# A hybrid recurrent and attention block: early loads at the turn, other places for gates and low parts, and another end

## The chip, the cores and the metric

The kernel runs on one core of one Trainium2 chip. The time is device time in microseconds (us) of one execution; lower is better. Engines are named as in the profile: PE (TensorE matmul), PEld (its weight loads), DVE (VectorE), ACT (ScalarE), POOL (GpSimd), SP (SyncE, here a queue for DMAs only). L154 is line 154 of the kernel before.

## The reference, cut to what matters

One block over 2048 rows of 1024 channels, in float32. From c come shift, scale and gate; h is the normed x. One input projection of h (1024 to 8192) gives eight parts; a recurrent branch and an attention branch each end in a 1024 x 1024 projection; they are merged by sigmoid gates, projected by w_o, added to x under the gate, and normed.

```python
mod = c_act @ w_mod[l] + b_mod[l]
shift, scale, gate = jnp.split(mod, 3, axis=-1)
h = rms_norm(x, g_norm[l]) * (1.0 + scale[:, None, :]) + shift[:, None, :]
x_rnn, z_rnn, q, k, v, z_attn, g_r, g_a = jnp.split(h @ w_in[l], IN_SPLITS, axis=-1)
...
y_rnn = (hr * jax.nn.silu(z_rnn)).astype(dt) @ w_out_rnn[l]
...
y_attn = (o * jax.nn.silu(z_attn)).astype(dt) @ w_out_attn[l]
merged = jax.nn.sigmoid(g_r + bg_r) * y_rnn + jax.nn.sigmoid(g_a + bg_a) * y_attn
x = x + gate[:, None, :] * (merged @ w_o[l])
...
return rms_norm(x, g_final)
```

The attention has 8 heads of 128 channels and three causal (window, dilation) sets, whose results are mixed by their softmax denominators.

## The kernel before, in words

**Products in three matmuls.** A float32 product is made of three matmuls on operands that were split into a high and a low part (`mm3`, L156; every matmul is recorded at L154 in `mm`): high by high, high by low, low by high. The high part is a copy on ACT (`hi_act`, L162). The low part is value minus high part, on POOL (`lo_pool`, L168) or DVE (`lo_dve`, L171). Tiles named yh and yl, kq, F and S hold such parts.

**The input projection** runs first, for each half of the rows in 28 pairs of column blocks, each pair as a Strassen-Winograd scheme of 7 products of 12 matmuls (128 x 512). Products go to the PSUM banks X, Z, W, V, Y; DVE and ACT take them from there. Results go to scratch arrays in DRAM: qT, kT, vN, yaT (the recurrent branch's result), grT and gaT (gates). A rotated pair of q or k (`rotated_pairs`) ends in a `store` of four DMAs for each result block, on SP (L1219); plain pairs store at L1249. `after_prod` is a table of functions to call after the n-th product. `output_weights` writes the split output weights to wD; `gated_weight` gates and combines parts of w_o and writes them to oD, on ACT's queue.

**The turn** is the place between the last product of the projection and the first work of the attention. Behind the last operands of the projection, `load_next` loads what the output projection begins with: weights S from wD (`load_wd`, L367), the first four k blocks of yaT's first 512 columns as 256 KB tiles R (`load_yd`, L373), and the other four as one 1 MB tile T (L345). All are on SP, in the order of the code; a tile of a ring (S has 4 here, R 4, T 14) is loaded once the tile that had the place is used up.

**The attention and its fill.** The work after the turn has an order written out by hand (`tc.manual_schedule`). It runs in slots of a `plan`; each slot makes the scores of one unit of a head, then softmax, transposes and sums. A head loads k and q in four parts (`load_kq`, L1571 and L1572, tiles kraw), splits them (`split_kq`: kq on ACT and POOL), and copies the queries of its windowed unit on POOL (`window_queries`, tile q, L1585). Between the attention's parts `spend` takes steps from the generator `steps`, which is the output projection of both branches: a step is one k block (`mm3`) of a tile (j, m), 512 columns j by 128 rows m of the output; a tile is 8 steps or 24 matmuls. How many steps are due is counted in `owed`. At the start of `steps`, `split_y(0, k)` splits the 8 blocks of the first y; a tile's result is multiplied by the sigmoid gate fg (`evict`, L1941; `load_g`, L1936) and stored to mrT or, summed with the recurrent branch's part, to meT.

**The end.** `output_products` opens when the attention is done. It takes the last 128 steps (two blocks of columns of the attention branch, whose first y comes from oT, tiles R). Beside them, at step numbers given by `at_step`, it loads 28 pieces of w_o (`load_o`), in the order B_ORDER of seven blocks of four, gates those that come from w_o itself (`gate_o`, L2069; those from oD are gated already), and splits them (`hi_o`, `lo_o`) into tiles F. The gate is broadcast to 128 rows in gate_b (L2052). Later pieces are handled in `jobs`, which are counted by products. Then each pair of 128-row groups takes a Strassen scheme of seven products with w_o (X, Z, W, V, Y again): `tt(u2, Z, u1)` and `tt(u3, W, u2)` on DVE (L2277, L2282), POOL adds them to the residual x (L2264, tile xo), and `finish` adds V, X or Y on DVE (L2235), which frees the bank. For the last group `finish_last` does it all without delay: squares on ACT, `first_root` (L2190, L2191), `last_root` (L2195 to L2198; a Newton step), the scaling, and output DMAs on SP (L2228).

## Time and profile before

| | us |
|---|---|
| median of 3 runs (lowest, highest) | 2195.78 (2193.06, 2198.0) |
| the profiled execution, its own time | 2195.18 |
| its span in the profile | 2193.4 |
| PE busy in it | 2156.6 |
| mean granted clock of PE | 0.996 |

The span runs from the first to the last record of the profiled execution; the execution's own time has 1.78 us around it. A row of the timeline gives start, duration, engine, line, operation, output<-input, shape, and in brackets how long the engine was idle ahead of it and what ended that. A row of the windows gives the busy time of PE, PEld, DVE, ACT and POOL in a stretch, then the clock that was granted to PE (1.00 is full speed), the mean busy share of the 16 DMA engines, and GB/s. In the chain of waits a piece stands with start, duration, and the engine or transfer that it followed. The lines themselves are in the prediction.

### The profile page before, as it was taken

To read this page: it belongs to the slowest core of one execution; us is meant where nothing else is said; L and a number is where in the kernel's file an instruction comes from. 1 tells how busy PE (TensorE), PEld (TensorE's weight loads), DVE (VectorE), ACT (ScalarE), POOL (GpSimd) and SP (SyncE) were. 2 spreads that over 40 slices of the span, in tenths; PEclk is the share of its full clock that TensorE was granted. 3 is DMA by queue.
4 is the path that set the end of the run, shared out by engine and by line. 5 is a ranking of instruction groups with operands and counts; after the bars stand their busy time and mean duration, and the time that the engine had idled before them with its cause. 6 is when DMAs were issued, how large, how long until landed. Compare 5 with 4: busy or idle time off the path is not lost.

```text
span 2193.4 us, 34275 instructions
## 1 busy us (share of the span) xinstructions
PE 2156.6 (98%) x11332; PEld 1833.7 (84%) x11333; DVE 1491.1 (68%) x2455; ACT 1261.4 (58%) x2543; POOL 1239.5 (57%) x910
## 2 busy tenths in 40 slices
PE   8999999999999999999999999999999999999998
PEld 6998888888888998888888887888889898978786
DVE  6769888978576765455545466466677878756876
ACT  4547667667543447557557412667678887633433
POOL 2467767677566355445445223446475656433986
PEclk9999999999999999999999999999999999999999
DMA  8355665665997568887887898989988888799553
GB/s 296 111 162 195 218 199 185 209 217 186 275 272 221 161 189 256 249 251 232 262 260 245 264 288 269 290 267 274 286 269 271 237 267 255 219 295 296 175 164 135
DMA packets 454522, 513.91 MB, mean 234 GB/s; under 512 B 91240, under 2 KB 333636, under 8 KB 453576
## 3 DMA queue, kind: packets, MB, share of 16 engines
q1 hardware_dynamic: 427444, 431.81, 65.8%
q10 hardware_dynamic: 26708, 79.86, 9.4%
q8 instruction: 90, 1.47, 0.3%
q14 instruction: 88, 0.72, 0.1%
q0 software_dynamic: 192, 0.05, 0.0%
HBM read 337.52 MB, written 174.07 MB: 233 GB/s over the span
## 4 chain that ended last, share of the span: by engine, by line
PE 60%; DMA 7%; DVE 4%; POOL 3%; issue 3%; SPq 1%; ACT 1%; POOLq 0%; ACTq 0%; DVEq 0%
PE X L154 12%; PE V L154 11%; PE pj L154 9%; PE W L154 7%; PE Z L154 7%; PE Y L154 6%; PE sc L154 3%; PE o L154 3%; PE pg L154 1%; DMA R<-oT 1%; DMA S<-wD 1%; PE pT L1708 1%; POOL kq L168 1%; DMA meT<-fg 1%; DMA fg<-mrT 1%
## 5 line engine op out<-in xcount | busy, mean ns | idle before, releaser
L168 POOL TENSOR_TENSOR S<-R,S 128x512 fp32r<-128x512 f32 x278 | 412.8, 1490 | 374.0 <-ACT S L162 294.6
L154 PE MATMUL V<-T,S 128*128 128x512 f32 x1344 | 324.4, 390 | 0.6 <-DVE xr L482 0.6
L154 PE MATMUL X<-T,S 128*128 128x512 f32 x1344 | 323.3, 389 | 0.3 <-POOL S L168 0.3
L154 PEld LDWEIGHTS X<-T,S 128*128 128x128 f32 x1344 | 252.0, 188 | 52.8 <-POOL S L168 0.7
L154 PEld LDWEIGHTS V<-T,S 128*128 128x128 f32 x1344 | 251.4, 188 | 53.0 <-DVE xr L482 1.0
L154 PE MATMUL pj<-yh,S 128*128 128x512 f32 x848 | 286.7, 395 | 4.9 <-ACT yh L162 4.3
L162 ACT ACTIVATE S<-R 128x512 fp32r<-128x512 f32 x278 | 171.2, 622 | 123.2 <-DMA R<-in_w_in_dram 85.0
L168 POOL TENSOR_TENSOR S<-s,S 128x512 fp32r<-128x512 f32 x114 | 184.6, 1619 | 99.8 <-ACT S L162 72.4
L154 PEld LDWEIGHTS pj<-yh,S 128*128 128x128 f32 x848 | 160.2, 189 | 37.9 <-ACT yh L162 5.2
L1624 ACT ACTIVATE pp<-pp,st 128x256 f32<-128x256 f32 (+3 forms) x256 | 133.4, 523 | 74.7 <-DVE st L1623 74.3
L154 PE MATMUL pj<-yl,S 128*128 128x512 f32 x424 | 167.2, 394 | 2.3 <-DVE yl L171 1.4
L154 PE MATMUL Y<-T,S 128*128 128x512 f32 x672 | 161.5, 389 | 0.0
L154 PE MATMUL W<-T,S 128*128 128x512 f32 x672 | 161.5, 389 | 0.0
L154 PE MATMUL Z<-T,S 128*128 128x512 f32 x672 | 161.4, 389 | 0.0
L154 PEld LDWEIGHTS Z<-T,S 128*128 128x128 f32 x672 | 126.1, 188 | 26.2
L154 PEld LDWEIGHTS Y<-T,S 128*128 128x128 f32 x672 | 126.1, 188 | 26.2
L154 PEld LDWEIGHTS W<-T,S 128*128 128x128 f32 x672 | 126.1, 188 | 26.1
L162 ACT ACTIVATE S<-s 128x512 fp32r<-128x512 f32 x114 | 71.1, 624 | 114.7 <-DVE s L299 68.2
L1026 DVE SCALAR_TENSOR_TENSOR xc<-xr,par,xc 128x512 f32<-128x512 f32 x96 | 97.0, 1010 | 52.7 <-ACT xc L1020 50.5
L171 DVE TENSOR_TENSOR ptl<-pT,pth 128x384 fp32r<-128x384 f32 (+1 forms) x160 | 97.8, 628 | 49.9 <-ACT pth L162 47.7
L1623 DVE CUSTOM_DVE_ANT_0 pp<-sc,msk 128x256 f32<-128x256 f32 (+3 forms) x256 | 104.2, 448 | 37.0 <-PE sc L154 34.8
L168 POOL TENSOR_TENSOR kq<-kraw,kq 128x512 fp32r<-128x512 f32 (+1 forms) x64 | 101.2, 1592 | 40.0 <-ACT kq L162 30.5
(397 smaller groups left out, 4822.5 us busy)
## 6 DMA issues: line engine op xcount, KB each, us to landing
sD<-S ACTq DMA_DIRECT2D x112, 512.0 KB, 3.7
S<-sD SPq DMA_DIRECT2D x112, 512.0 KB, 4.9
S<-wD SPq DMA_DIRECT2D x100, 512.0 KB, 6.0
R<-in_w_in_dram SPq DMA_DIRECT2D x195, 256.0 KB, 4.3
wD<-s ACTq DMA_DIRECT2D x64, 256.0 KB, 4.7
T<-in_w_mod_dram SPq DMA_DIRECT2D x8, 1024.0 KB, 10.3
vN<-ev SPq DMA_DIRECT2D x64, 128.0 KB, 2.8
zaT<-ev SPq DMA_DIRECT2D x32, 256.0 KB, 3.6
```

What stands on the lines that cost most here:

```text
L154: nc.tensor.matmul(o, lhsT=l, rhs=r, start=st, stop=sp, **kw)
L162: nc.scalar.activation(o, i, AF.Copy)
L168: nc.gpsimd.tensor_tensor(o, i, h.bitcast(F32), ALU.subtract)
L171: nc.vector.tensor_tensor(o, i, h.bitcast(F32), ALU.subtract)
L1026: nc.vector.scalar_tensor_tensor(xc, xr[:, i : i + CH], cw(i), xc, ALU.mult, ALU.add)
L1623: nc.vector.tensor_tensor_reduce(pdst, s_ps, mask, 1.0, 3e38, ALU.add, ALU.min, m_)
L1624: nc.scalar.activation(pdst, pdst, AF.Exp, bias=m_, scale=-1.0, accum_out=l_)
L1708: nc.tensor.transpose(pt[:, c0 + j * P : c0 + (j + 1) * P], pp[i][:, k * P : (k + 1) * P], ident)
```

## The change

Four parts.

1. **The turn.** The mixed loads of the first y (four R, one T) become `load_first_y`: two loads of 1 MB into tiles T, called when seven products of the projection are still to come, and so queued ahead of the weights S. The stores of the rotated q and k of the second half go to ACT's queue instead of SP's. The first output tile does its 16 matmuls on yh first and its 8 on yl behind them. Two of its low parts (k = 0 and 2) go from DVE to POOL. Six steps of the fill are taken before the first slot, and `owed` starts at -6.
2. **gate_b** is loaded at step 48 of `output_products` instead of step 3. In B_ORDER the block B11 goes from the first place to the fourth, so that the first three blocks come from oD and need no gate.
3. **Gates and low parts.** The gates of pieces 24 to 26 are called at steps 118, 120 and 122 instead of as jobs behind the first products; the low parts of pieces 21, 23 and 26 go from POOL to DVE.
4. **The end.** EPS is added by a small DVE step right after the first square; the root is taken on ACT from the two sums at once (one as its bias), while DVE sums them; `last_root` has three steps instead of four and gives half the value, so gf is doubled once on ACT. One of the last group's output DMAs goes to ACT's queue.

The diff, cut to its core:

```diff
@@ load_next
             if k < 3:
                 load_wd(0, 0, k) if k < 2 else load_wd(0, 1, 0)
-            if k < 4:
-                load_yd(yaT, 0, k)
-            if k == 1:
-                t = T(hp, [P, KH, CH], F32, "T", bufs=14)
-                nc.sync.dma_start(t[:], yaT[KH * P :, :CH].rearrange("(k p) j -> p k j", p=P))
...
+    def load_first_y():
+        for half in range(2):
+            t = T(hp, [P, KH, CH], F32, "T", bufs=14)
+            nc.sync.dma_start(t[:], yaT[half * KH * P : (half + 1) * KH * P, :CH].rearrange("(k p) j -> p k j", p=P))
+            for i in range(KH):
+                Y0[True, 0, half * KH + i] = t[:, i, :]
@@ rotated_pairs, store
-                        nc.sync.dma_start(dstT[r0 : r0 + 32, :, n * P : (n + 1) * P],
+                        (nc.scalar if f else nc.sync).dma_start(dstT[r0 : r0 + 32, :, n * P : (n + 1) * P],
@@ the projection's last stage
         if f:
             gated_weight(qp)
+            after_prod.setdefault(2 * 28 * 7 - 7, []).append(load_first_y)
@@ steps
-                on_dve = k not in (3, 4) if j == LAST_HEAD else k % 2 or not j
+                on_dve = k not in (3, 4) if j == LAST_HEAD else k % 2 or not j and k > 2
...
-                mm3(ps[:], wt[:, 0, row % KH, :], wt[:, 1, row % KH, :], yh[:], yl[:], first=k == 0, last=k == KT - 1)
+                ws = [wt[:, i, row % KH, :] for i in range(2)]
+                if t:
+                    mm3(ps[:], *ws, yh[:], yl[:], first=k == 0, last=k == KT - 1)
+                else:
+                    for i in range(2):
+                        mm(ps[:], ws[i], yh[:], k == i == 0, False)
+                    low.append((ws[0], yl))
+                while low and k == KT - 1:
+                    wh, yl = low.pop(0)
+                    mm(ps[:], wh, yl[:], False, not low)
@@ output_products
-        at_step(3, lambda: nc.sync.dma_start(gate_b[:], gateD[0:1, :].broadcast_to([P, D])))
+        at_step(48, lambda: nc.sync.dma_start(gate_b[:], gateD[0:1, :].broadcast_to([P, D])))
...
-            (lo_dve if i % 2 and i // KH != 5 else lo_pool)(F[name][1][:, k, :], raw_o.pop(i), F[name][0][:, k, :])
-        B_ORDER = "B11", "T2", "T3", "T1", "B21", "T4", "B22"
+            (lo_dve if i % 2 or i == 26 else lo_pool)(F[name][1][:, k, :], raw_o.pop(i), F[name][0][:, k, :])
+        B_ORDER = "T2", "T3", "T1", "B11", "B21", "T4", "B22"
...
             at_step(57 + 2 * i, lambda i=i: load_o(i))
+            at_step(70 + 2 * i, lambda i=i: gate_o(i))
...
-            for d, fn in ((1, gate_o), (2, hi_o), (3, lo_o)):
+            for d, fn in ((1, gate_o), (2, hi_o), (3, lo_o))[i < 27 :]:
...
+        soon(5, lambda: nc.scalar.activation(gf[:], gf[:], AF.Copy, scale=2.0))
@@ first_root, last_root
-            nc.vector.tensor_scalar(ss[:, 0], ss[:, 0], ss[:, 3], EPS, ALU.add, ALU.add)
-            nc.scalar.activation(ss[:, 1], ss[:, 0], AF.Sqrt)
+            nc.scalar.activation(ss[:, 1], ss[:, 3], AF.Sqrt, bias=ss[:, 0])
+            nc.vector.tensor_tensor(ss[:, 0], ss[:, 0], ss[:, 3], ALU.add)
...
-            nc.vector.reciprocal(y, y)
-            nc.vector.tensor_scalar(t, y, y, v, ALU.mult, ALU.mult)
-            nc.vector.tensor_scalar(t, t, -0.5, 1.5, ALU.mult, ALU.add)
-            nc.vector.tensor_scalar(y, y, t, None, ALU.mult)
+            nc.vector.reciprocal(t, y)
+            nc.vector.tensor_scalar(t, t, v, y, ALU.mult, ALU.add)
+            nc.vector.reciprocal(y, t)
@@ finish_last, finish
+            if not whole:
+                nc.vector.tensor_scalar(ss[:, 0], ss[:, 0], EPS, None, ALU.add)
...
-                    nc.sync.dma_start(outv[n, r + i][:, q * CH : (q + 1) * CH], v)
+                    (nc.scalar if q == 1 - j and not i else nc.sync).dma_start(outv[n, r + i][:, q * CH : (q + 1) * CH], v)
@@ the slots
-        owed = 0.0
+        for _ in range(6):
+            next(fill)
+            n_steps[0] += 1
+        owed = -6.0
```

What that does to the order of the instructions is shown at three places. The first is SP's queue at the turn, before (kT are stores of k; S<-wD weights, R and T the first y, msk the attention's masks, kraw its k and q, fg a gate; L1219 rotated stores, L1249 plain ones):

```order
L1219 DMA kT<-t_2301_12723 128x1x128 x4
L1249 DMA kT<-t_2308_12775 384x1x128
L1249 DMA kT<-t_2308_12775 128x1x128
L1249 DMA kT<-t_2312_12817 128x1x128
L1249 DMA kT<-t_2312_12817 384x1x128
L367 DMA S_2317_12842<-wD 128x1024
L373 DMA R_2318_12844<-yaT 128x512
L367 DMA S_2319_12846<-wD 128x1024
L373 DMA R_2320_12848<-yaT 128x512
L345 DMA T_12850<-yaT 128x4x512
L367 DMA S_2324_12867<-wD 128x1024
L373 DMA R_2325_12869<-yaT 128x512
```

And of the changed kernel, where L1248 are the plain stores, L366 the weights and L345 the new loads:

```order
L1248 DMA kT<-t_2308_12775 384x1x128
L1248 DMA kT<-t_2308_12775 128x1x128
L345 DMA T_12797<-yaT 128x4x512
L345 DMA T_12799<-yaT 128x4x512
L1248 DMA kT<-t_2314_12821 128x1x128
L1248 DMA kT<-t_2314_12821 384x1x128
L366 DMA S_2319_12846<-wD 128x1024
L366 DMA S_2320_12848<-wD 128x1024
L366 DMA S_2323_12865<-wD 128x1024
L366 DMA S_2387_13041<-wD 128x1024
```

The whole first y is now asked for ahead of all weights, and the rotated stores have left this queue. The second place is further down on the same queue, the first loads of the attention. Before:

```order
L1536 DMA msk_13007<-in_cst_dram 128x896
L1571 DMA kraw_13056<-kT 128x256
L1572 DMA kraw_13056<-qT 128x256
L1571 DMA kraw_13059<-kT 128x256
L1572 DMA kraw_13059<-qT 128x256
L1936 DMA fg_13062<-grT 128x512
L367 DMA S_2394_13070<-wD 128x1024
L1571 DMA kraw_13078<-kT 128x256
L1572 DMA kraw_13078<-qT 128x256
```

In the changed kernel:

```order
L1936 DMA fg_13047<-grT 128x512
L1536 DMA msk_13001<-in_cst_dram 128x896
L366 DMA S_2389_13053<-wD 128x1024
L1571 DMA kraw_13057<-kT 128x256
L1572 DMA kraw_13057<-qT 128x256
L1571 DMA kraw_13060<-kT 128x256
L1572 DMA kraw_13060<-qT 128x256
L1571 DMA kraw_13065<-kT 128x256
L1572 DMA kraw_13065<-qT 128x256
```

The first gate fg and one set of weights have moved ahead of k and q. The order of the matmuls changes in the first output tile alone (its yl behind its yh).

The third place is DVE's queue where the products with w_o begin (gates L2069, sums of operands L2132 to L2144, u L2277 and L2282, xo L2235, low parts L171). Before:

```order
L2144 TENSOR_TENSOR s_4100_21439<-R_4096_21404,s_4100_21439 128x512
L2069 TENSOR_TENSOR rw_21379<-rw_21379,gate_b_20752 128x512
L2069 TENSOR_TENSOR rw_21390<-rw_21390,gate_b_20752 128x512
L2069 TENSOR_TENSOR rw_21402<-rw_21402,gate_b_20752 128x512
L2277 TENSOR_TENSOR u_4126_21575<-Z_21551,u_4120_21549 128x512
L2132 TENSOR_TENSOR s_4128_21591<-R_4110_21487,R_4114_21520 128x512
L2133 TENSOR_TENSOR s_4129_21592<-s_4128_21591,R_4105_21463 128x512
L171 TENSOR_TENSOR F_21570<-rw_21390,F_21569 128x512
L2069 TENSOR_TENSOR or_21499<-or_21499,gate_b_20752 128x512
L2282 TENSOR_TENSOR u_4131_21602<-W_21578,u_4126_21575 128x512
L2142 TENSOR_TENSOR R_4110_21487<-R_4105_21463,R_4110_21487 128x512
L2235 TENSOR_TENSOR xo_21527<-V_21606,xo_21527 128x512
```

In the changed kernel (L2154 is the sum that was L2144; L2291 and L2296 are u, L2247 xo):

```order
L171 TENSOR_TENSOR F_21473<-or_21416,F_21472 128x512
L2154 TENSOR_TENSOR s_4097_21433<-R_4093_21398,s_4097_21433 128x512
L2291 TENSOR_TENSOR u_4123_21569<-Z_21546,u_4117_21544 128x512
L2142 TENSOR_TENSOR s_4125_21585<-R_4107_21484,R_4111_21517 128x512
L2143 TENSOR_TENSOR s_4126_21586<-s_4125_21585,R_4102_21459 128x512
L171 TENSOR_TENSOR F_21565<-rw_21384,F_21564 128x512
L2078 TENSOR_TENSOR or_21496<-or_21496,gate_b_20746 128x512
L2296 TENSOR_TENSOR u_4128_21596<-W_21572,u_4123_21569 128x512
L2152 TENSOR_TENSOR R_4107_21484<-R_4102_21459,R_4107_21484 128x512
L171 TENSOR_TENSOR F_21565<-rw_21396,F_21564 128x512
L2247 TENSOR_TENSOR xo_21524<-V_21600,xo_21524 128x512
```

The three gates of rw stand further up, ahead of two evictions of yh; one low part is new between the sum R and xo, and two more (one is the first row here) stand ahead of the place.

More of the change, by code (lines that the diff above doesn't have):

```diff
@@ L339, in load_next @@
                 load_wd(0, 0, k) if k < 2 else load_wd(0, 1, 0)
-            if k < 4:
-                load_yd(yaT, 0, k)
-            if k == 1:
-                t = T(hp, [P, KH, CH], F32, "T", bufs=14)
-                nc.sync.dma_start(t[:], yaT[KH * P :, :CH].rearrange("(k p) j -> p k j", p=P))
-                for i in range(KH):
-                    Y0[True, 0, KH + i] = t[:, i, :]
+    def load_first_y():
[4 more added lines that the diff above has]
+                Y0[True, 0, half * KH + i] = t[:, i, :]
     def load_free():
@@ L1952, in steps @@
         yield
-        last = None
+        last, low = None, []
         for t, (j, m) in enumerate(tiles):
@@ L2246, in square @@
                 nc.scalar.activation(jk[:], xo[:, cols], AF.Square, scale=D ** -0.5, accum_out=ss[:, 3 if whole else 0])
+                if not whole:
+                    nc.vector.tensor_scalar(ss[:, 0], ss[:, 0], EPS, None, ALU.add)
             def scale(q):
```

## The prediction, written before the changed kernel had run

> **What bounds the kernel now.** The page's first part is read first.
>
> ```profile
> PE 2156.6 (98%) x11332; PEld 1833.7 (84%) x11333; DVE 1491.1 (68%) x2455; ACT 1261.4 (58%) x2543; POOL 1239.5 (57%) x910
> ```
>
> TensorE is busy 2156.6 of 2193.4 us, no other engine above 68%. So an edit is worth only what it takes out of PE's idle time, out of the stretches at half clock that can follow such idle time, or out of the few us behind the last matmul. The change takes no matmul away. The next view is PE's waits by what they waited for (us in total, times, the longest).
>
> ```profile
> PE pj L154 <- ACT yh L162: 4.3, 2, 3.5
> PE V L154 <- DVE xo L2235: 2.7, 1, 2.7
> PE sc L154 <- POOL q L1585: 1.9, 5, 0.7
> ```
>
> Two places lie where the diff is: the turn (pj waits for yh, sc for q) and one V of the output products that waits for xo. A third, the first tile that needs the attention's o, shows in the timeline below. Each is priced from its own stretch: the timeline gives start, duration and, in brackets, the wait ahead; PEclk in a stretch is the granted clock.
>
> **The turn.** PE and the granted clock there (window; PE, PEld, DVE, ACT, POOL busy; clock, DMA share, GB/s):
>
> ```profile
> 1353.00 0.39 PE L154 MATMUL pj<-yh,S 128*128 128x512 f32 x1
> 1359.49 0.80 PE L154 MATMUL pj<-yh,S 128*128 128x512 f32 x1 [3.48 <-ACT yh L162]
> 1365.53 0.62 PE L154 MATMUL pj<-yh,S 128*128 128x512 f32 x2
> 1376.45 2.00 PE L154 MATMUL sc<-kq,q 128*128 128x128 f32 x12 [0.23 <-POOL q L1585]
> 1348.00:1353.00 5.00, 5.00 (x23) 4.13 (x22) 0.69 (x1) 0.99 (x2) 0.00 (x0) 1.00 1.03 410
> 1356.70:1363.50 6.80, 4.01 (x9) 2.90 (x10) 3.79 (x6) 3.34 (x6) 0.00 (x0) 0.50 1.02 305
> ```
>
> A matmul of this shape follows the last after 0.227 us where nothing is waited for (pairs 0.46 apart). The first tile has 24, so it is worth 5.44 us; it starts at 1353.00 and the next one starts with the second matmul of the row at 1365.53, at 1365.76. It took 12.76, 7.3 too long: waits, and a clock of 0.50 behind them. At 1376.45 the first windowed scores wait another 0.23. So if nothing were late, those scores would start 7.5 us earlier, at 1368.9. The chain of waits (start, duration, what) names the cause:
>
> ```profile
> 1342.42 5.81 DMA S<-wD
> 1348.25 10.54 DMA R<-yaT
> 1363.30 4.52 DMA kraw<-kT
> 1367.84 5.91 DMA kraw<-qT
> 1374.54 1.30 POOL kq L168
> 1375.84 1.12 POOL q L1585 x2
> ```
>
> The timeline has the stores and the engines that make hi parts (yh, ACT) and low parts (yl, DVE):
>
> ```profile
> 1336.44 2.50 SPq L1219 DMA_DIRECT2D kT<-t  x4
> 1353.81 0.63 ACT L162 ACTIVATE yh<-R 128x512 fp32r<-128x512 f32 x1 [2.46 <-DMA R<-yaT]
> 1359.99 2.18 ACT L162 ACTIVATE yh<-T 128x512 fp32r<-128x512 f32 x4
> 1353.20 0.69 DVE L482 TENSOR_TENSOR t<-V,u 128x512 f32<-128x512 f32 x1 [2.03 <-PE V L154]
> 1360.78 2.49 DVE L171 TENSOR_TENSOR yl<-T,yh 128x512 fp32r<-128x512 f32 x4
> ```
>
> The chain's R<-yaT pieces were queued on SP behind the weights and then shared a full DMA (share 1.03) with the loads around it: 10.5 us for 256 KB. Shortly before, the DMA engines were not full:
>
> ```profile
> 1337.00:1342.00 5.00, 5.00 (x24) 4.14 (x23) 5.00 (x4) 0.63 (x1) 5.00 (x4) 1.00 0.63 144
> ```
>
> The two new 1 MB loads go into that gap: they need slots that are free once seven products are left (7 x 12 x 0.227 = 19 us ahead of 1353, 1334), and SP reaches them after fewer stores, about 1337. Two MB is 5 us at the full 410 GB/s and more over the spare 0.37; I take 6 to 10: in by 1347. The hi parts then wait only for their own memory (shared with weight blocks that are still being written out, and free by the hi part of 1353.81 at the latest) and for ACT, eight at 0.55 us (2.18 over 4); DVE follows with t<-V to 1353.9 and six low parts of 0.62 (2.49 over 4), to 1357.6, POOL does two of 1.3 (as its kq). PE runs 16 matmuls on hi parts to 1356.6 and the 8 low ones to 1358.4: the tile stalls 0 to 1.3 us. That the hi products go first costs nothing: same 24 matmuls.
>
> **What is late next** is the attention. In before, kraw<-kT waited at 1363.30 for the slot of the last yl, then for a landing at 1367.82 before the next pair's q could be issued, landed 1373.75, ACT and POOL followed, and the scores at 1376.45. With yl done 5.7 us sooner (1357.6 against 1363.3) the chain shifts by up to 5.7. But fg, msk and a 512 KB S<-wD now stand ahead of the first kraw on SP: two more issues of some 0.4 us and more bytes in a full DMA, about 1.1 us in all. The scores come at 1371.8, 2.9 after what PE could do. **Gain 4.6**, between 2.5 (that new wait of 3 brings its own half clock, 2 us) and 7.5 (no wait).
>
> The moved q and k stores: SP paid 2.50 us for four, mostly queue time. ACT now pays it, 32 times 0.6, about 20 us of the last stretch in front of the turn, where it was busy 0.63 of 5.00. Behind a store in ACT's queue stand the hi parts and copies that the last products need; I price that at 0, and at 1 us per product pair as the end, because ACT is idle most of that stretch and its last hi parts came with about 1 us to spare. Taking the six fill steps ahead changes no PE order, only the order of the loads that is counted above.
>
> **gate_b.** The tile that needs o:
>
> ```profile
> 1947.30 2.20 PE L154 MATMUL Z<-F,S 128*128 128x512 f32 x9
> 1950.59 0.50 PE L154 MATMUL Z<-F,S 128*128 128x512 f32 x1 [1.09 <-ACT F L162]
> 1957.17 1.09 PE L154 MATMUL W<-F,S 128*128 128x512 f32 x4
> 1940.27 0.32 SPq L2052 DMA_DIRECT2D gate_b<-gateD  x1
> 1942.64 2.56 SPq L373 DMA_DIRECT2D R<-oT  x2
> 1940.00:1950.00 10.00, 8.68 (x36) 6.42 (x35) 2.42 (x4) 1.99 (x4) 2.57 (x2) 1.00 1.02 366
> ```
>
> It took 9.87 (1947.30 to 1957.17) for 5.44 of work. DMA is full at 366 GB/s, and gate_b writes 128 x 1024 x 4 bytes, 0.52 MB, ahead of R<-oT: 1.4 us of transfer; its issue and the queue places behind it are some 0.8 more. The loads of o come 2.2 sooner, and every wait in the tile is downstream of them: **2.2**, between 0.8 (the later pieces are bound by POOL's and DVE's low parts) and 3.5. At step 48 gate_b is one of many loads, and the blocks that now come first in the order need no gate; 0.
>
> **Gates sooner, three low parts to VectorE.**
>
> ```profile
> 2049.85 4.86 PE L154 MATMUL V<-F,S 128*128 128x512 f32 x12 [2.69 <-DVE xo L2235]
> 2054.55 1.75 PE L154 MATMUL Z<-F,S 128*128 128x512 f32 x7
> 2034.75 5.20 DVE L2069 TENSOR_TENSOR rw<-rw,gate_b 128x512 f32<-128x512 f32 x3
> 2046.67 0.68 DVE L2282 TENSOR_TENSOR u<-W,u 128x512 f32<-128x512 f32 x1
> 2049.10 0.69 DVE L2235 TENSOR_TENSOR xo<-V,xo 128x512 f32<-128x512 f32 x1 [1.16 <-POOL xo L2264]
> 2034.70:2047.40 12.70, 12.46 (x55) 9.92 (x53) 12.61 (x11) 4.30 (x7) 11.50 (x7) 1.00 0.57 187
> 2047.00:2054.50 7.50, 4.71 (x13) 3.20 (x13) 5.75 (x8) 5.28 (x13) 7.07 (x5) 0.77 0.55 176
> ```
>
> V waits 2.69 for a bank, and its 12 matmuls then take 4.70 (2049.85 to 2054.55) instead of 12 x 0.227 = 2.72: 1.98 more at a clock of 0.77 over the window. Together 4.67. DVE is busy 12.61 of 12.70 ahead of it; three gates (5.20, 1.73 each) head the queue, so u<-W is done late, at 2047.35, POOL's xo<-xo,u after it and DVE's xo<-V last, 1.75 behind u<-W. The change takes the three gates out of that queue and adds two low parts of the same size ahead of it (3.5, some 1.4 of which falls into idle time) and one between R<-R,R and xo<-V, beside POOL's step. u<-W starts 5.2 - 2.1 = 3.1 sooner, 2043.6, and ends 2044.3; POOL's step is through at 2046.0, R<-R,R (as u<-W, 0.68) and the added low part (1.73) at 2046.7, xo<-V at 2047.4. PE wants the bank at 2049.85 - 2.69 = 2047.16: 0.3 is left. **Gain 4.4**, between 1.5 (half the wait and the clock stay) and 4.9 (all of it and POOL's relief).
>
> Here the clock is a price of its own. By the Trainium skill, "TensorE: Matmul & The Clock Gate", section "HAM oscillation", the rule is "no PE-idle gaps >~3.4µs"; by it a gap of 2.69 would cost only itself, the slow V would have another cause, and this term would be 2.7, the sum 1.7 less. The row decides otherwise: 0.77 was granted right behind 2.69.
>
> **The end.** Behind the last matmul:
>
> ```profile
> 2187.24 0.20 DVE L2190 TENSOR_SCALAR ss<-ss 128x1 f32<-128x1 f32 x1
> 2187.72 0.16 DVE L2195 RECIPROCAL ss<-ss 128x1 f32<-128x1 f32 x1 [0.27 <-ACT ss L2191]
> 2188.71 0.72 ACT L2223 ACTIVATE xo<-xo,ss 128x512 f32<-128x512 f32 x1 [1.03 <-DVE ss L2198]
> 2189.84 0.42 SPq L2228 DMA_DIRECT2D out_dram<-u  x1
> ```
>
> The DVE step ahead of the root goes (0.20 and the hop to ACT), but a sum on DVE now runs beside the root, so 0.2 to 0.4; four steps from 2187.72 to 2188.7 become three, 0.25; u's DMA waits until 2189.84 behind xo's on one queue, and with two the last issue is xo's, when ACT is done at 2189.43: 0.4. **1.0**, between 0.5 and 1.5. The doubling of gf on ACT is done long before: 0.
>
> **The sum.** 4.6 + 2.2 + 4.4 + 1.0 = 12.2 us. The profiled execution took 2195.18 (span 2193.4 and 1.78 around it), 0.6 below the median of 2195.78: 2195.18 - 12.2 = **2183.0**.
>
> **Rivals.**
> 1. The attention's loads come in time. The DMA has spare room before 1348, and all SP stores of the second half's q and k are gone from in front of them. Then the turn gives 7.5: 2180.1. Against it: the last kraw pair waits for slots and landings, not for SP alone. 0.12.
> 2. The turn gives nothing: the loads of the attention, not the output tile, set the scores at 1376.45, because the DMA is full (1.02) through the tile and bytes are not fewer. 2187.6. For it: the chain goes through kraw from 1363.30; against it, that kraw waited for yl. 0.17.
> 3. DVE's backlog only moves: the low parts put on DVE run 1.73 beside POOL and V still waits. 2187.4. 0.08.
> 4. V's slow 1.98 is not the gap's. The window's 0.77 has another cause and stays, the term is 2.7: 2184.7. 0.05. By the Trainium skill's rule above it would go this way.
> 5. The other side: the stores on ACT wait in its queue, and hi parts and copies of the last products stand behind them. A burst of four stores on SP took as long as 4.69:
>
> ```profile
> 1319.91 4.69 SPq L1219 DMA_DIRECT2D kT<-t  x4
> ```
>
> One such burst ahead of a hi part, less 1 us of slack, is 3.7 of PE's time and 2.0 of half clock; in three of the last pairs 17. It decides from 12.2 us on, that is where all three have it: 2200. Against it: in before, ACT has 4 us free of 5 in this stretch, and landings are quick while DMA is at 0.63. 0.06.
>
> **How the numbers follow.** Forecast 0.52, rivals 0.12, 0.17, 0.08, 0.05 and 0.06. The forecast's own range is 2178.5 to 2188. What a measurement can tell from no change is about 0.2%, 4.4 us, so faster means below 2191.4. The forecast and rivals 1 to 4 all lie below it when they come alone; of rivals 2 and 3 (0.25) I take 0.1 for the case where a second term fails too and the time comes within 0.2%. Faster 0.84, same 0.10, slower 0.06. The range: all terms at their upper ends are 17.4, 2177.8; upward it takes in rivals 2 and 3 with a second term short, 2191.
>
> **What would show it.** Turn right: no wait above 1 us in the first tile and clock 1.0 there, and a new wait of 1 to 4 us of sc for q or kq. Wrong: waits of X or V for S, T or t in the last 30 us ahead of the turn (rival 5), or pj still waiting for yh. gate_b right: the Z tile at some 7.7 instead of 9.87. Gates right: that V without a wait above 0.8 and its twelve matmuls in 2.7. End right: the root without a DVE step ahead of it, and the last output DMA issued 1 us sooner behind the last matmul. What would make the sum wrong most is a load order at the turn that I read as hidden and that is not.

## The result, and the profile after

| | before | after |
|---|---|---|
| median (lowest, highest; 9 runs each), us | 2195.78 (2192.11, 2198.45) | 2189.84 (2186.10, 2191.36) |
| ratio of after to before, 95% interval | | 0.9971 (0.9963 to 0.9979) |
| the profiled execution, its span, us | 2195.18, 2193.4 | 2191.29, 2189.4 |

The change is faster, by 0.29%: 6 us, half of the 12.2 that were forecast, and inside the stated range. One run of e16 (2251.71 us, at a mean granted clock of 0.913 where all others have 0.99 or more) was slow, and all medians and ratios here are without it. PE's waits of the changed kernel (total, times, longest), to set against those of before:

```profile
PE sc L154 <- POOL q L1585: 2.6, 5, 0.7
PE Z L154 <- ACT F L162: 2.3, 3, 1.6
PE V L154 <- DVE xo L2247: 2.2, 1, 2.2
PE pj L154 <- ACT yh L162: 0.8, 1, 0.8
```

Of the 4.3 us in which pj waited for yh, the 3.5 at the turn are gone; the 0.8 that is left comes near 1940 us, before and after. But V still waits 2.2 for xo, and Z has a new wait of 1.6. PE's timeline at the turn:

```profile
1352.97 3.90 PE L154 MATMUL pj<-yh,S 128*128 128x512 f32 x16
1356.71 2.42 PE L154 MATMUL pj<-yl,S 128*128 128x512 f32 x8
1358.97 0.39 PE L154 MATMUL pj<-yh,S 128*128 128x512 f32 x1
1370.24 2.00 PE L154 MATMUL sc<-kq,q 128*128 128x128 f32 x12 [0.69 <-POOL q L1585]
```

The first tile takes 6.0 us (1352.97 to 1358.97) instead of 12.8, and the scores start at 1370.24 instead of 1376.45. And where the products with w_o begin:

```profile
2022.37 2.88 PE L154 MATMUL X<-F,S 128*128 128x512 f32 x12
2026.88 3.00 PE L154 MATMUL Z<-F,S 128*128 128x512 f32 x12 [1.63 <-ACT F L162]
2030.60 3.01 PE L154 MATMUL W<-F,S 128*128 128x512 f32 x12 [0.72 <-DVE fg L1941]
2046.73 4.60 PE L154 MATMUL V<-F,S 128*128 128x512 f32 x12 [2.24 <-DVE xo L2247]
2051.17 2.89 PE L154 MATMUL Z<-F,S 128*128 128x512 f32 x12
```

In before X, Z, W and V followed each other every 2.72 us here. Now Z and W wait, and V with its slow matmuls is nearly as it was (4.44 to the next Z, 4.70 before).

The time went, stretch by stretch, as the next table shows. It is worked out from the starts of the same matmuls in the traces: change of each stretch's length against before, in us (negative is shorter). "Z, W, V" runs from the first product X to the first product V; "V again" from the X that opens the next pair of row groups (called the second X here, 2044.25 in before) to the Z behind it; the 8.2 us between the two are the same in all.

| stretch (start in before) | before, us | after | e1 turn | e2 gate_b | e3 gates | e5 late gates |
|---|---|---|---|---|---|---|
| to the first output tile (0) | 1353.0 | 0.0 | 0.5 | 0.4 | -0.5 | 2.0 |
| first tile to scores (1353.0) | 23.5 | -6.2 | -4.9 | -0.3 | -1.2 | -4.9 |
| attention (1376.5) | 570.9 | 1.1 | 1.5 | -0.5 | 0.0 | 0.8 |
| tile that needs o (1947.3) | 9.9 | -0.4 | 0.4 | -1.0 | -0.1 | -0.5 |
| rest of the fill (1957.2) | 70.8 | 0.0 | 0.0 | 0.0 | 0.0 | 0.0 |
| Z, W, V (2027.9) | 8.2 | **2.9** | 0.0 | **7.1** | 0.1 | **3.4** |
| V again (2044.3) | 10.3 | -0.7 | 0.4 | -2.0 | -2.7 | 1.1 |
| rest (2054.6) | 138.8 | -0.6 | -0.3 | 0.0 | 0.0 | -0.3 |
| span | 2193.4 | -3.9 | -2.5 | 3.7 | -4.4 | 1.5 |

The first row is nearly the same program in all of these kernels; its differences of up to 2 us, and some of 1 to 2 us in the attention, are what two executions differ by; the tile that needs o is 0.4 shorter in this execution of the changed kernel and 2.1 in another (e14). So a stretch at a wait tells more than the span of one execution, and for the whole the medians and their ratios are used.

### The profile page after: what moved, and what is told of

It is laid out like the page before. It is cut to its first block, busy times and chain, and to the rows that moved or that the text cites. A ratio compares the mean times of both kernels' runs of the same rounds, so it can differ in the third digit from the quotient of the medians.

```text
span 2189.4 us, 34270 instructions
## 1 busy us (share of the span) xinstructions
PE 2156.2 (98%) x11333; PEld 1834.3 (84%) x11333; DVE 1494.8 (68%) x2456; ACT 1266.5 (58%) x2544; POOL 1237.3 (57%) x909
## 4 chain that ended last, share of the span: by engine, by line
PE 62%; DMA 8%; DVE 5%; issue 2%; ACT 2%; POOL 1%; SPq 1%; DVEq 0%; ACTq 0%; POOLq 0%
PE X L154 12%; PE V L154 11%; PE pj L154 9%; PE W L154 6%; PE Z L154 6%; PE Y L154 6%; PE sc L154 4%; PE o L154 4%; PE pg L154 1%; DMA vraw<-vN 1%; PE pT L1708 1%; PE pT L1721 1%; DMA mrT<-fg 1%; DMA or<-in_w_o_dram 1%; DMA or<-oD 1%
## 5 line engine op out<-in xcount | busy, mean ns | idle before, releaser
L171 DVE TENSOR_TENSOR ptl<-pT,pth 128x384 fp32r<-128x384 f32 (+1 forms) x160 | 97.8, 628 | 50.8 <-ACT pth L162 48.6
L1688 ACT ACTIVATE pp<-pp,M 128x256 f32<-128x256 f32 (+3 forms) x256 | 118.6, 528 | 9.2 <-DVE M L1812 9.2
```

Of the source, the lines that this page charges most:

```text
L171: nc.vector.tensor_tensor(o, i, h.bitcast(F32), ALU.subtract)
L1688: nc.scalar.activation(pp, pp, AF.Copy, scale=w)
```

## The experiments

The first four runs take parts of the change alone, or one part out. The theories: "paced" says that a lead of PE is lost again, because loads set the later waits; "moved work", that the gates were put ahead of evictions; "added terms" is the prediction's own sum.

**e1, the turn alone** (before, with the first part of the diff).

> The first part of the change alone (the turn), on the kernel before. Theory 'paced': from about 1955 to 2030 us the DMA engines are full, the operands of the products with w_o and DVE's queue follow the loads, and a lead that PE has won upstream is lost at the first V that waits for xo. Then PE leads by 5 to 6 us until the last tile of the fill, that V waits 4 to 5.5 us instead of 2.69, and the span gains 1 to 3 us. Theory 'added terms' (what the prediction did): the lead of about 5 is kept, V waits 2.69 as before, and the span gains 4.6 to 5.2.

Ratio 0.9971 (0.9959 to 0.9983). PE leads by 4.5 us at the scores, 3.0 at the tile that needs o, 2.6 at the first product X, and 2.6 at the end; V's wait does not grow:

```profile
2047.56 3.25 PE L154 MATMUL V<-F,S 128*128 128x512 f32 x7 [2.72 <-DVE xo L2244]
2050.99 1.49 PE L154 MATMUL V<-F,S 128*128 128x512 f32 x5 [0.18 <-POOL F L168]
```

"Paced" falls in the form in which it was stated: a lead that PE has at the products goes on. The span gains 2.6 in this execution, less than "added terms" had (4.6 to 5.2), the medians 6.5. (The second row has a short wait for a low part on POOL inside V; it comes up again in e12.)

**e2, gate_b and the order of blocks alone.**

```diff
-        at_step(3, lambda: nc.sync.dma_start(gate_b[:], ...))
+        at_step(48, lambda: nc.sync.dma_start(gate_b[:], ...))
-        B_ORDER = "B11", "T2", "T3", "T1", "B21", "T4", "B22"
+        B_ORDER = "T2", "T3", "T1", "B11", "B21", "T4", "B22"
```

> The second part alone: gate_b loaded at step 48 and the block B11 loaded fourth. Prediction's step: the tile that waits for R<-oT is 2.2 us shorter and the span gains 2.2. Theory 'paced': that tile gains 0.4 to 1 (it did 0.4 with the whole change), and the 0.52 MB that now stand in the full stretch make the later loads and V's release 1 to 1.7 later, so the span gains nothing or is up to 1.5 us longer.

Ratio 1.0010 (1.0001 to 1.0020): alone, this part makes the kernel slower. Its timeline (PE, then DVE and SP) shows how:

```profile
2033.41 5.46 PE L154 MATMUL Z<-F,S 128*128 128x512 f32 x12 [4.00 <-DVE yh L1941]
2032.57 0.69 DVE L1941 TENSOR_TENSOR yh<-Z,yh 128x512 f32<-128x512 f32 x1 [4.16 <-DMA yh<-gaT]
2024.84 0.32 SPq L1936 DMA_DIRECT2D yh<-gaT  x1
```

The second product wants the bank Z, which holds a tile of the fill until DVE has multiplied it by its gate; DVE stands idle for 4.16 us until that gate has landed, 7.6 us after its issue. Behind this wait Z's 12 matmuls are slow (5.46 us, at a granted clock of 0.50), which is most of the rest of the 7.1. Before's DVE and SP timelines, and its window for the stretch ahead of that place:

```profile
2028.16 0.69 DVE L1941 TENSOR_TENSOR yh<-Z,yh 128x512 f32<-128x512 f32 x1 [2.88 <-PE W L154]
2021.67 0.32 SPq L1936 DMA_DIRECT2D yh<-gaT  x1
```

```profile
1960.00:2028.00 68.00, 68.00 (x302) 56.31 (x301) 41.63 (x51) 21.30 (x36) 25.43 (x18) 1.00 0.99 299
```

In before the eviction waits for its gate as well, though the row names PE: Z's tile was done at 2022.65, and the gate, issued at 2021.67, landed 6.4 us later, at 2028.07. The bank is free at 2028.85, 1.8 us ahead of need (2030.65).

For 68 us the DMA engines are busy 0.99, at 299 GB/s. By the bytes alone, 0.52 MB more would cost a load behind them about 1.7 us (an estimate, 0.52 MB at 299 GB/s). Measured against PE's need the gate lands 5.8 later: from 2.6 ahead to 3.2 behind. Most of that is a later issue: SP comes to this load 9.0 us ahead of the need in before and 4.4 in e2.

**e3, gates sooner and three low parts on DVE, alone.**

```diff
-            (lo_dve if i % 2 and i // KH != 5 else lo_pool)(F[name][1][:, k, :], ...)
+            (lo_dve if i % 2 or i == 26 else lo_pool)(F[name][1][:, k, :], ...)
             at_step(57 + 2 * i, lambda i=i: load_o(i))
+            at_step(70 + 2 * i, lambda i=i: gate_o(i))
-            for d, fn in ((1, gate_o), (2, hi_o), (3, lo_o)):
+            for d, fn in ((1, gate_o), (2, hi_o), (3, lo_o))[i < 27 :]:
```

> The third part alone: gates of pieces 24 to 26 sooner, low parts of 21, 23 and 26 on DVE. Theory 'moved work': the gates stand in DVE's queue ahead of the evictions of the last two tiles of the fill, and the products that want those banks (Z, W) wait 1 to 2.7 us, whatever lead PE has. Theory 'paced': without a lead from upstream DVE gets to the evictions in time, Z and W wait less than 0.5, V is released about 3 us sooner and its wait of 2.69 and the slow matmuls behind it go: gain 3.5 to 4.7, as the prediction's step had it.

Ratio 0.9967 (0.9953 to 0.9981). No wait of Z or W, although the gates stand ahead of the evictions (yh<-Z and fg<-W); V still waits 1.5, so the stretch gains 2.7 and not 3.5 to 4.7, and its matmuls are no longer slow:

```profile
2047.29 3.03 PE L154 MATMUL V<-F,S 128*128 128x512 f32 x12 [1.52 <-DVE xo L2236]
```

**e5, the changed kernel with the gates late again.**

```diff
-            at_step(70 + 2 * i, lambda i=i: gate_o(i))
-            for d, fn in ((1, gate_o), (2, hi_o), (3, lo_o))[i < 27 :]:
+            for d, fn in ((1, gate_o), (2, hi_o), (3, lo_o)):
```

> The changed kernel with the gates of pieces 24 to 26 back behind the first products (the three low parts stay on DVE). Theory 'paced': Z and W wait 2.3 us less, but V waits that much more, since its release hangs on the loads and DVE's sum of work: the span is as the changed kernel's within 1 us, or longer. Theory 'moved work': Z and W do not wait, V's wait stays at 2.2, the span is 2 to 2.7 us shorter than the changed kernel's.

Ratio 0.9976 (0.9966 to 0.9985). Z and W wait all the same (3.4), and V longer (3.16). So the gates' new place isn't what delays Z and W. "Moved work" falls, and so does "paced", by which Z and W were to wait less; what e2 and e5 have in common with the changed kernel is the load of gate_b and the order of blocks.

The next four tell these two apart, and try a version without them.

**e6, the changed kernel with gate_b at step 3.**

```diff
-        at_step(48, lambda: nc.sync.dma_start(gate_b[:], ...))
+        at_step(3, lambda: nc.sync.dma_start(gate_b[:], ...))
```

> The changed kernel with gate_b loaded at step 3 again; B_ORDER stays new. After the first four runs the theory is 'late loads': the 0.52 MB of gate_b stand at step 48 in a stretch of 70 us in which the DMA engines are full, every load behind them is about 2 us later, and the gate values of the last two tiles of the fill land too late for their evictions, so that the products Z and W wait for these banks. By it, Z and W do not wait here (less than 0.3 us together, where the changed kernel has 2.8 more than before), and from the first Z tile to the product V the kernel is as long as before. Rival 'order of blocks': loading B11 fourth does it, and the waits of 1 to 4 us stay.

Ratio 0.9963 (0.9950 to 0.9976). Z does not wait, W 0.4; the stretch Z, W, V is 0.8 longer than before, not 2.9:

```profile
2024.37 2.98 PE L154 MATMUL Z<-F,S 128*128 128x512 f32 x12
2027.74 3.00 PE L154 MATMUL W<-F,S 128*128 128x512 f32 x12 [0.40 <-DVE fg L1941]
2043.61 3.06 PE L154 MATMUL V<-F,S 128*128 128x512 f32 x12 [1.11 <-DVE xo L2247]
2046.50 2.88 PE L154 MATMUL Z<-F,S 128*128 128x512 f32 x12
```

The order of the blocks is left with that 0.8, a little above what was expected for "late loads". V comes out better too (-2.5 in the stretch "V again"): DVE, which was late by the evictions, is not late any more. And the tile that needs o is no longer here (-0.6) than in the changed kernel (-0.4), though gate_b is loaded ahead of R<-oT again (in e15, the same kernel, -0.2).

**e7, the whole second part undone:** the edit of e6, and

```diff
-        B_ORDER = "T2", "T3", "T1", "B11", "B21", "T4", "B22"
+        B_ORDER = "B11", "T2", "T3", "T1", "B21", "T4", "B22"
```

> The changed kernel without its second part (gate_b at step 3 and B11 first again). Both theories: no wait of Z or W. By the stretches of the single parts: turn -5 (to 1939), gates -2.7 to -4, end -0.6, so 8 to 9.5 us shorter than before, 2 to 3 us shorter than the changed kernel.

Ratio 0.9963 (0.9951 to 0.9976), the same as e6: Z, W, V as in before, V again -3.8. (Its profiled execution is the fastest of its six and 13.1 shorter than before's, 2.6 of it in the attention.)

**e8, the changed kernel without the bytes of gate_b.**

```diff
-        at_step(48, lambda: nc.sync.dma_start(gate_b[:], ...))
+        at_step(48, lambda: nc.gpsimd.memset(gate_b[:], 1.0))
```

> The changed kernel with gate_b filled with ones on GpSimd at step 48 instead of its load; this leaves out the gate on the blocks B11, B21 and B22 of w_o. 'Late loads': without the bytes Z and W do not wait, the first Z tile keeps the gain of 0.4 to 1, and the span is 2.5 to 4 us shorter than the changed kernel's. 'Order of blocks': the waits stay.

Ratio 0.9962 (0.9949 to 0.9975). Z waits 0.24 and W 0.48, in the stretch 1.2 instead of 2.9; the tile that needs o is 1.4 shorter than in before. The bytes are most of it, the new order some.

**e9, e7 with the bank V copied on ACT,** a version that the profile of e7 points to.

```diff
+            v1 = V
+            if not x:
+                v1 = T(gp, [P, CH], F32, "v1", bufs=1)
+                nc.scalar.activation(v1[:], V[:], AF.Copy)
-            finish(x, 1, 1, V, u3)
+            finish(x, 1, 1, v1, u3)
```

> The kernel without the second part (as e7) and, for the first group of rows, a copy of the bank V on ScalarE from which xo is formed, so that the bank is free without VectorE. If V's wait is VectorE's backlog alone, the wait for xo is gone (was 1.5 to 2.2) and the V product starts at once; what then ends last is the low part of piece 27 for its last three matmuls (0 to 1.5 us). Then 1 to 3 us shorter than e7. If the copy itself stands behind other work on ScalarE or GpSimd's operands are late, no gain.

Ratio 0.9966 (0.9950 to 0.9982): no gain. The bank is free at once, but the last two matmuls wait 1.58 instead, behind DVE:

```profile
2042.18 2.43 PE L154 MATMUL V<-F,S 128*128 128x512 f32 x10
2046.19 0.73 PE L154 MATMUL V<-F,S 128*128 128x512 f32 x2 [1.58 <-DVE ss L2260]
2042.70 1.76 DVE L2247 TENSOR_TENSOR xo<-v,xo 128x512 f32<-128x512 f32 x1 [2.44 <-POOL xo L2278]
2044.39 1.75 DVE L171 TENSOR_TENSOR F<-or,F 128x512 fp32r<-128x512 f32 x1
```

The low part of piece 27 (F<-or) stands behind an addition that waits 2.44 for POOL; the page names the small step ss behind it, which is the next on DVE, but it is F that the matmul reads.

**e10, the same with that addition behind the next product.**

```diff
+            if not x:
+                v1 = T(gp, [P, CH], F32, "v1", bufs=1)
+                nc.scalar.activation(v1[:], V[:], AF.Copy)
+                product(X, "B21", False, True, 7 * x + 4)
+                finish(x, 1, 1, v1, u3)
```

> As e9 (no second part, the bank V copied on ScalarE for the first group), and that group's addition of V to xo comes behind the next product, so that the low part of piece 27 stands ahead of it in VectorE's queue. Theory: with the bank free and the low part early, nothing of the V product waits more than 0.5 us (e9 lost 1.6 to the low part, e7 0.7 to the bank). The stretch from the second X to the second Z is 5.4 to 6 us, against 6.5 in e7 and 9.6 in the changed kernel; the span 0.5 to 1.5 us under e7's, about 0.4% under before.

Ratio 0.9953 (0.9941 to 0.9966), the lowest of all. V waits 0.64, for the low part alone:

```profile
2041.04 2.43 PE L154 MATMUL V<-F,S 128*128 128x512 f32 x10
2044.11 0.74 PE L154 MATMUL V<-F,S 128*128 128x512 f32 x2 [0.64 <-DVE F L171]
2044.69 3.12 PE L154 MATMUL Z<-F,S 128*128 128x512 f32 x12
```

From the second X (2038.32) to the second Z it takes 6.37, a little more than expected and near e7's 6.46; and 1.2 are lost again in the next groups, to waits of up to 0.6. So the wait went where it was meant to go, but the traces show no gain of this edit over e7, only the medians do, by 2 us, and those are of two sessions.

**e11, the bytes alone:** e7 with a copy of 0.52 MB that nothing needs.

```diff
+        spare = scratch("spareD", [P, D])
+        at_step(48, lambda: nc.sync.dma_start(spare[:, :], w_o[0, :P, :]))
```

> The kernel without the second part (e7) with a copy of 0.52 MB from one place in DRAM to another, which nothing needs, at step 48: the bytes of gate_b alone, without its order and without its users. 'Late loads' through bytes: the products Z and W wait 1 to 5 us together, as with gate_b there. If not the bytes but gate_b's own place did it (its gates late, its broadcast), no wait, and the span is as e7's within 1 us.

Ratio 0.9967 (0.9955 to 0.9979). Z and W wait again, and without gate_b or the new order:

```profile
2023.34 2.99 PE L154 MATMUL Z<-F,S 128*128 128x512 f32 x12 [0.45 <-ACT F L162]
2027.09 3.00 PE L154 MATMUL W<-F,S 128*128 128x512 f32 x12 [0.77 <-DVE fg L1941]
```

The stretch Z, W, V is 1.8 longer; in the nine traces with gate_b at step 3, the old order and no copy, before among them, it is within 0.4. So a transfer of that size at that place is enough for a wait, though not for the 2.9 to 7.1 with gate_b and the new order. The times don't tell e11 from e7 (0.9967 and 0.9963, in two sessions).

**e12, the gates sooner without the low parts on DVE:** e7, and

```diff
-            (lo_dve if i % 2 or i == 26 else lo_pool)(F[name][1][:, k, :], ...)
+            (lo_dve if i % 2 and i // KH != 5 else lo_pool)(F[name][1][:, k, :], ...)
```

> The kernel without the second part (e7) with the three low parts back on GpSimd: the gates sooner alone. If the low part of piece 26 on GpSimd is a second bound of the V product (the chain of before ends in it), V starts as in e7 or sooner, and its last six matmuls wait 0.5 to 2 us for that low part: the stretch from the second X to the second Z is 1 to 2.5 us longer than e7's. If the gates did all, it is the same within 0.4.

Ratio 0.9977 (0.9968 to 0.9987).

```profile
2042.20 1.88 PE L154 MATMUL V<-F,S 128*128 128x512 f32 x7 [1.52 <-DVE xo L2247]
2045.64 1.42 PE L154 MATMUL V<-F,S 128*128 128x512 f32 x5 [1.55 <-POOL F L168]
2046.90 2.89 PE L154 MATMUL Z<-F,S 128*128 128x512 f32 x12
```

The gates alone give 1.2 in the stretch "V again", e7 3.8. V still takes 4.70 (2042.20 to 2046.90), as in before, but here at full rate: seven matmuls, then 1.55 of waiting for POOL's low part. The slow V of before had two bounds at once: before's chain of waits goes through that low part, which ends at 2053.22, and V's last five matmuls start at 2053.28.

**e13, e7 with the rotated stores back on SP.**

```diff
-                        (nc.scalar if f else nc.sync).dma_start(dstT[...], ...)
+                        nc.sync.dma_start(dstT[...], ...)
```

> The kernel without the second part (e7) with the rotated stores back on SP's queue, so that the loads of y stand behind them. If the early loads need the move, y comes 3 to 6 us later, the first tile waits again and the scores come 2 to 6 us later than in e7. If they don't (SP reaches them in time either way), the scores come as in e7 within 0.7 us, and the move of the stores to ScalarE does nothing for the time.

Ratio 0.9984 (0.9975 to 0.9994). The scores come at 1374.15, 4.0 later than in e7, but not for y. PE's waits:

```profile
PE pj L154 <- DMA S<-wD: 2.4, 2, 1.5
PE sc L154 <- POOL kq L168: 1.0, 1, 1.0
```

The first tile wants its weights, which SP issued late; y was there. In this execution the move of the stores is worth 4.0 of e7's 6.3 us by the scores, by what it frees on SP for the weights and for k and q.

This run shows something else: without the second part V again gains only 1.0 here. V waits 2.00, and its matmuls take 4.4.

**e14, e15, e16: the changed kernel, e6's and e10's, in one session.**

> The changed kernel itself, in one session with the next two: 0.3% under before, as on record.

> The changed kernel with gate_b at step 3 (the kernel of e6). 'Late loads': 2 to 5 us under the changed kernel in the same session, and no wait of Z and W over 0.8 us together. If the place of gate_b matters little, within 1 us.

> The kernel of e10 (no second part, copied bank, late addition): 4 to 6 us under the changed kernel in the same session, 1 to 2.5 us under e15.

| | median, us | ratio to before (95%) | Z, W, V against before | V again |
|---|---|---|---|---|
| e14, the changed kernel | 2189.87 | 0.9977 (0.9966 to 0.9987) | 5.0 | -3.1 |
| e15, gate_b at step 3 | 2187.54 | 0.9963 (0.9950 to 0.9975) | 1.1 | -2.5 |
| e16, no second part, bank V copied | 2185.52 | 0.9959 (0.9945 to 0.9973) | 0.4 | -4.9 |

gate_b's place alone is 2.3 us between the medians of e14 and e15; the intervals of e15 and e16 still overlap e14's a little. e16, the kernel of e10, is 4.4 under the changed kernel and faster than before by 0.41%; it came out lowest in both of its sessions. Against e15 its 2.0 are not clear: the intervals overlap, and of the 4.9 in the stretch of V, 1.3 are lost again behind it (a Z that waits 0.93 for POOL's low part). In e14, Z and W lose more than in the first profile (Z waits 3.18, and its matmuls take 4.58) and V less: PE comes later to V, and so waits less there (1.07).

## Why the prediction was wrong

**The turn: right.** 4.6 was forecast; by the scores it is 6.2, and 5.1 are left when the attention ends (it took 1.1 longer, no more than two executions differ by). The early y, the first tile at full clock (1.00 from 1353 to 1360; in e1 one wait of 1.07 for yh is left in it) and a last wait of the scores for q came as written; that last wait is 0.7 us, and the scores come 1.3 behind 1368.9, what PE could do by the forecast, not 2.9. The early part that was costed at nothing, the move of the stores to ACT, is what a good part of the gain hangs on (e13, one execution: 4.0 us), through the weights; ACT was not held up by them.

**gate_b's gain: wrong size.** "The loads of o come 2.2 sooner" was taken from the bytes ahead of them. With gate_b out of their way the tile is 0.4 to 2.1 shorter (after, e2, e5, e8, e14; 1.1 in the mean); with gate_b ahead of them it goes from 0.3 longer to 2.2 shorter (e11), 0.3 shorter in the mean of the eleven runs. So some 0.7 is left, and one execution can't show it. In the changed kernel's first profile the first wait is 0.9 shorter, and the rest follows low parts and later loads:

```profile
1942.17 2.20 PE L154 MATMUL Z<-F,S 128*128 128x512 f32 x9
1944.57 0.49 PE L154 MATMUL Z<-F,S 128*128 128x512 f32 x1 [0.19 <-ACT F L162]
1946.69 0.96 PE L154 MATMUL Z<-F,S 128*128 128x512 f32 x3 [0.44 <-POOL F L168]
1950.33 0.51 PE L154 MATMUL Z<-F,S 128*128 128x512 f32 x1 [0.52 <-ACT F L162]
1951.63 0.63 PE L154 MATMUL W<-F,S 128*128 128x512 f32 x2
```

The first wait went from 1.09 to 0.19, but the tile ends 9.46 after its start: the 0.5 at 1950.33 is new, and stands behind the last load of o. The working had named the lower bound of 0.8 for such a reason, and not taken it.

**gate_b's new place: the step that failed.** The prediction said "At step 48 gate_b is one of many loads, and the blocks that now come first in the order need no gate; 0." The prediction shows no window of that place. The DMA engines are full there for 68 us, and the load makes the gates of the last tiles come later than PE wants their banks. What followed is 2.9 us in the stretch Z, W, V (5.0 in e14, 7.1 in e2). SP's and DVE's rows of the changed kernel:

```profile
1971.30 0.93 SPq L2061 DMA_DIRECT2D gate_b<-gateD  x1
2026.05 0.69 DVE L1941 TENSOR_TENSOR yh<-Z,yh 128x512 f32<-128x512 f32 x1
```

Z's wait of 1.63 is put down to ACT's F, done at 2026.77; this Z reads blocks that were split long before, and the bank is freed by this yh<-Z at 2026.74, whose gate landed at 2025.9. The same reading of every trace (us; the need is the start of the first X and 2.72) gives:

| second part | runs | the gate of Z's tile lands | the bank is free | Z waits |
|---|---|---|---|---|
| none | before, e1, e3, e7, e9, e10, e12, e13, e16 | 1.6 to 4.4 ahead of need | 0.7 to 3.0 ahead | no |
| the new order alone | e6, e8, e15 | 0.5 to 1.0 ahead | 0.2 ahead to 0.3 behind | 0 to 0.24 |
| a transfer at step 48 alone | e11 | 0.7 ahead | 0.5 behind | 0.45 |
| both | after, e14, e5, e2 | 0.8, 2.2, 1.1, 3.2 behind | 1.65, 3.2, 1.9, 4.0 behind | 1.63, 3.18, 1.87, 4.00 |

Z's wait is in each of them the lateness of its bank. The order and the transfer each take about 2 us of a lead of 2.7 (means of the rows), both together 4.5; only then does the gate itself come too late, and slow matmuls behind the wait can come on top (in e2 and e14, above). So the new order, which the prediction also put at 0, costs as much of the lead as the transfer. Through which waits of SP's queue a transfer 50 us earlier makes the gate's issue late, no run follows.

**The gates and low parts: right mechanism, overtaken.** Forecast 4.4, of which 0.7 came. The same edit gives 2.7 (e3), 2.5 (e6) and 3.8 (e7) without late evictions, but 1.0 in e13 without them and 3.1 in e14 with them, so this stretch alone doesn't say what the second part took. With Z, W, V put to it, the changed kernel loses 2.2 against before (1.9 in e14), and the kernels with the third part and without the second gain 1.0 to 3.8 (e3, e7, e13): the second part costs 3 to 6 here. How much of the missing 3.7 is its doing stays open; the rest is size, for V still waits 0.7 to 2.0 without it. The working's 1.98 for "a clock of 0.77" was a half truth. At half clock V's matmuls hid a second bound, POOL's low part of piece 26; e12 keeps the 4.70 without any half clock (1.00 from 2042 to 2047). The term was right only because the change moved that low part as well.

**The end:** 0.6 in this profile instead of 1.0, of which e1 has 0.4 without this part. The root is shorter by 0.5 as forecast (from the last square to the scaling 1.89 us instead of 2.41). But the addition ahead of it, xo<-pj, comes 0.5 later behind the last matmul's start, since the other row group's new sum on DVE took 1.01 us instead of the 0.21 of the step that it replaced (it ended at 2182.17, POOL's product xo<-xo,gf beside it at 2182.16; e14 has the same 1.01):

```profile
2181.16 1.01 DVE L2202 TENSOR_TENSOR ss<-ss 128x1 f32<-128x1 f32 x1 [1.18 <-ACT ss L2201]
2182.67 0.67 DVE L2213 TENSOR_TENSOR xo<-pj,xo 128x512 f32<-128x512 f32 x1
```

What is left is the second queue: the last output DMA is issued 0.36 sooner behind the last matmuls.

**The sum.** By the profiled execution: turn -5.1, tile -0.4, Z, W, V +2.9, V -0.7, end -0.6: -3.9. Of the forecast's 12.2, 1.8 were lost in the tile, 2.9 to new waits, 3.7 in the V stretch, 0.4 at the end, and the turn gave 0.5 more. By the medians the change gave 5.9. With part two undone, the timed ratio is 0.9963, 8.1 us, without either of its new waits. The measured 2189.84 lies above the forecast's own range (2178.5 to 2188); the stated one held it, by luck, because it went up to 2191 for other cases, rivals 2 and 3 with a second term short. The rival that came nearest in kind, a backlog that "only moves" (2187.4), had 0.08, and its cause was another one than the rival named.

**The rival on the other side** (ACT blocked by stores) did not show: in the 30 us ahead of the turn PE's timeline has no wait in the changed kernel.

## What to carry to other kernels

When a load is moved, its new place needs the same reading as its old one: the DMA share of the stretch that it moves into, what is queued behind it, and by how much the first of those lands ahead of need. Where the DMA engines were full here, what was put in was paid by a load with a small margin, the gate of an eviction 55 us further on. And where a slow stretch is explained by one bound, look for the next one at the same time: a wait behind a slow clock doesn't show.

## What the runs showed of the hardware that was not expected

The clock after a gap. Behind PE's gap of 2.69 (before) and of 2.24 (after), half clock was granted for some 3 us (0.53 and 0.63 in the mean of the next 3.4 us); behind 1.52 (e3) and 1.63 (after) none (1.00). Behind 2.00 in e13 the clock was 0.50 over the next 3.4 us, behind 2.06 at the same place in e15 it stayed 1.00. Behind the same gap of 2.04 it was granted once and once not; windows of before, then of after:

```profile
1829.00:1832.40 3.40, 3.13 (x24) 2.90 (x25) 1.60 (x9) 3.40 (x12) 1.29 (x1) 1.00 0.03 9
```

```profile
1823.80:1827.20 3.40, 3.13 (x20) 2.94 (x21) 1.69 (x9) 3.40 (x11) 1.29 (x1) 0.78 0.06 21
1827.20:1830.60 3.40, 3.40 (x13) 2.96 (x13) 2.92 (x8) 3.40 (x9) 2.54 (x2) 0.72 0.66 171
```

The gap ends at 1828.91 in before and at 1823.80 in after. So near 2 us it depends on more than the gap's length. The prediction weighed the rule of the Trainium skill ("TensorE: Matmul & The Clock Gate", section "HAM oscillation", gaps over about 3.4 us) against one row; the runs bear the row out at 2.00, 2.24 and 2.69.
